# Attention over short sequences: working 32 heads at a time instead of 16, with 8 KB runs for Q, K and the output

## The chip, the cores and the metric

The kernel runs on one core of a Trainium2 chip. The metric is the device time of one execution in microseconds, given as the median of several executions.

## The reference

There are 32 x 12 = 384 independent heads. Each has Q, K and V of 128 rows by 64 columns in f32. For each head the output is softmax(Q K^T / 8) V, with the softmax taken along the rows:

```python
scale = 1.0 / np.sqrt(q.shape[-1])
scores = scale * np.matmul(q, k.transpose(0, 1, 3, 2))
scores_max = np.max(scores, axis=-1, keepdims=True)
attn = np.exp(scores - scores_max)
attn = attn / (np.sum(attn, axis=-1, keepdims=True) + 1e-8)
return np.matmul(attn, v).astype(np.float32)
```

Q, K and V are 12.6 MB each and the output is 12.6 MB, all of it moved once. The kernels here leave the maximum out (the scores are small) and divide by the sum at the end.

## The kernel before

A **chunk** is 16 heads; there are 24 chunks. A chunk of Q is loaded as 128 partitions of `TQ` = 16 rows each, so each partition reads one contiguous run of 16 x 64 f32 = 4 KB. These loads come from GpSimd's queue (line 58 for Q and K), which turns f32 into bf16 on the way, so that 2 KB is written for each run of 4 KB. V is loaded by line 65, in runs of 2 KB, 32 heads for each DMA. Only the first chunk's Q and K come as f32 over the SP and ACT queues (line 81) and are cast by VectorE and ScalarE (line 83).

The steps for chunk c are these:

- `turn` (lines 107 and 109, VectorE): 32x32 block transposes put the head dimension of Q and K on the partitions. A pair of bf16 values is moved as one f32, so one chunk is 512 columns for each of Q and K.
- `scores` (line 120, TensorE, 32 matmuls) into `s_ps`, which is one slot of four PSUM banks, and the exponential of all 2048 columns (line 124, ScalarE) into `attn`.
- `values` (line 139, TensorE, then a copy by ScalarE, line 143): V's rows are brought into the order that the turned keys have, by matmuls with a permutation matrix `perm`.
- `denominators` (line 149) and `divide` (lines 171 and 173): sums over the keys by a matmul with ones, turned back by a VectorE transpose, and the reciprocal.
- `outputs` (line 159, twice per chunk, 16 matmuls each) and `finish` (line 178, VectorE): the transposed output in PSUM is turned back into `o_sb`.
- `scale_rows` (line 183, GpSimd): `o_sb` times the reciprocal. For the last chunk VectorE takes half (line 186).
- `store` (line 191): `o_sb` to HBM in runs of 4 KB, issued by ScalarE's queue, and by SP's for the last three chunks.

`d_ps`, `o_ps` and `v_ps` share `w_ps`: four slots of one PSUM bank.

The order of the instructions on each engine is written out by hand (`tc.manual_schedule()`); each engine works through its own list in order, and waits on semaphores for the others. The GpSimd queue uses eight semaphores in turn for its loads, so a load waits until the one eight before it has landed. Loads run `AHEAD` = 7 chunks ahead, and stores are held back by `LAG` = 9 chunks (the list `held`), so that the loads come first and the stores follow when the loads thin out. The main loop:

```python
for c in range(NCH):
    todo = shuffles.get(c, [])
    if c < e:
        turn(c + 1, 0)
        turn(c + 1, 1)
    d_ps = denominators(c)
    if c < e:
        scores(c + 1)
    divide(c, d_ps)
    finish(c, 0, outputs(c, 0))
    ...
```

The functions that the change touches:

Of the kernel before, what the change touches and what calls it, by code (L numbers as in the profile page):

```python
# [10 lines left out]
def kernel(  # L11
# [10 lines left out]

    nc = tc.nc
    f32 = mybir.dt.float32
# [5 lines left out]
    TQ = 16  # L30
    GQ = S // TQ
# [3 lines left out]
    NCH = B * H // 16  # L35
    AHEAD = 7
    LAG = 9
# [8 lines left out]
    pin = ctx.enter_context(tc.tile_pool(name="pin", bufs=AHEAD + 3))  # L46
    pt = ctx.enter_context(tc.tile_pool(name="pt", bufs=3))
    pa = ctx.enter_context(tc.tile_pool(name="pa", bufs=3))
    pf = ctx.enter_context(tc.tile_pool(name="pf", bufs=8))
# [5 lines left out]
    def load_qk(c):  # L55
        for src, which in ((qr, 0), (kr, 1)):
            x = pin.tile([128, TQ, D], bf16, tag="qk"[which] + "_bf", name="qk"[which] + "_bf")
            nc.gpsimd.dma_start(out=x, in_=src[:, c, :].rearrange("p (t d) -> p t d", t=TQ))  # L58
            chunks[c, which] = x
# [9 lines left out]
    with tc.manual_schedule():  # L69
        early = {0: 0, 1: 1, 2: 2, 3: 3, 4: 4, 5: 5}  # L70
        early.update({4 * m - 5 + i: 2 * m + i for m in range(3, NCH // 4) for i in range(2)})

        def load(c):
            load_qk(c)
            if c in early:
                load_v(early[c])

        for src, which, eng, cast in ((qr, 0, nc.sync, nc.vector.tensor_copy),
                                      (kr, 1, nc.scalar, nc.scalar.copy)):
            raw = po.tile([128, TQ, D], f32, tag="o_sb", name="raw")  # L80
            eng.dma_start(out=raw, in_=src[:, 0, :].rearrange("p (t d) -> p t d", t=TQ))
            x = pin.tile([128, TQ, D], bf16, tag="qk"[which] + "_bf", name="qk"[which] + "_bf")
            cast(x, raw)  # L83
            chunks[0, which] = x
        load_qk(1)
        load_v(early[0])
        ident = singles.tile([128, 128], bf16)
        make_identity(nc, ident)
        load_v(early[1])
        perm = singles.tile([128, A, 2, 32], bf16)  # L90
        nc.vector.memset(perm, 0.0)
        for tl in range(2):
            nc.vector.tensor_copy(
                perm[:, :, tl, tl * 16:(tl + 1) * 16].rearrange("p a (x g) -> p a x g", x=2),
                ident.rearrange("p (a g x) -> p a x g", a=A, x=2))
        ones = singles.tile([128, 32], bf16)
        nc.vector.memset(ones, 1.0)
        for c in range(2, AHEAD):
            load(c)

        def turn(c, which):


            x = chunks.pop((c, which)).bitcast(f32)
            xt = pt.tile([128, 4, S], f32, tag="qk"[which] + "t", name="qk"[which] + "t")
            if which == 0:
                nc.vector.transpose(xt.rearrange("p h (x g) -> p x h g", g=GQ), x)  # L107
            else:
                nc.vector.transpose(xt.rearrange("p h (x g) -> p x h g", g=GQ),  # L109
                                    x.rearrange("p (y t) e -> p t y e", y=2))  # L110
            qts[c, which] = xt.bitcast(bf16).rearrange("p h (s j) -> p h s j", j=2)

        def scores(c):
            qt, kt = qts.pop((c, 0)), qts.pop((c, 1))
            s_ps = ps.tile([128, 4, 4, S], f32, tag="s_ps", name="s_ps")
            for h in range(4):
                for j in range(2):
                    for b in range(4):
                        pr = slice(b * 32, (b + 1) * 32)
                        nc.tensor.matmul(  # L120
                            s_ps[:, b, h, :], lhsT=kt[pr, h, :, j], rhs=qt[pr, h, :, j],
                            start=(j == 0), stop=(j == 1), tile_position=(b * 32, 0))
            attn = pa.tile([128, 4, 4, S], bf16, tag="attn", name="attn")
            nc.scalar.activation(out=attn, in_=s_ps, func=mybir.ActivationFunctionType.Exp,  # L124
                                 bias=0.0, scale=scale)
            attns[c] = attn

        def values(m, a, heads, half):


            v_bf = chunks[m, 2]
            ns = slice(0, 2 * CB) if half is None else slice(half * CB, (half + 1) * CB)
            if m not in v2s:
                v2s[m] = pa.tile([128, A, 2 * CB, D], bf16, tag="v2", bufs=2, name="v2")
            v_ps = ps.tile([128, heads, 2 * CB // heads, D], f32, tag="w_ps", bufs=4, name="v_ps")
            for i in range(heads):
                for tl in range(2):
                    for u in range(4):
                        nc.tensor.matmul(  # L139
                            v_ps[u * 32:(u + 1) * 32, i], lhsT=perm[:, a + i, tl, :],  # L140
                            rhs=v_bf[:, ns, 2 * u + tl, :], start=(tl == 0), stop=(tl == 1),
                            tile_position=(0, u * 32))
            nc.scalar.copy(v2s[m][:, a:a + heads, ns], v_ps)  # L143

        def denominators(c):

            d_ps = ps.tile([128, 4, S], f32, tag="w_ps", bufs=4, name="d_ps")
            for b in range(4):
                nc.tensor.matmul(  # L149
                    d_ps[b * 32:(b + 1) * 32], lhsT=ones, rhs=attns[c][:, b],  # L150
                    start=True, stop=True, tile_position=(0, b * 32))
            return d_ps

        def outputs(c, j):

            o_ps = ps.tile([128, 4, S], f32, tag="w_ps", bufs=4, name="o_ps")
            for h in range(4):
                for b in range(4):
                    nc.tensor.matmul(  # L159
                        o_ps[b * 32:(b + 1) * 32, h],  # L160
                        lhsT=v2s[c // 4][:, 4 * (b % 2) + h, 2 * (c % 4) + b // 2,
                                         j * 32:(j + 1) * 32],
                        rhs=attns[c][:, b, h], start=True, stop=True, tile_position=(0, b * 32))
            return o_ps

        def turned(src):
            return src.rearrange("p h (x g) -> p x h g", g=GQ)

        def divide(c, d_ps):
            dt = pf.tile([128, TQ, 32], f32, tag="dt", name="dt")  # L170
            nc.vector.transpose(dt, turned(d_ps))  # L171
            recip = pf.tile([128, TQ], f32, tag="recip", name="recip")
            nc.vector.reciprocal(recip, dt[:, :, 0])  # L173
            osbs[c] = (po.tile([128, TQ, D], f32, tag="o_sb", name="o_sb"), recip)

        def finish(c, j, o_ps):
            o_sb, _ = osbs[c]
            nc.vector.transpose(o_sb[:, :, j * 32:(j + 1) * 32], turned(o_ps))  # L178

        def scale_rows(c):  # L180
            o_sb, recip = osbs[c]
            if c < NCH - 1:
                nc.gpsimd.tensor_mul(o_sb, o_sb, recip.to_broadcast([128, TQ, D]))  # L183
            else:
                for eng, sl in ((nc.gpsimd, slice(0, 32)), (nc.vector, slice(32, 64))):
                    eng.tensor_mul(o_sb[:, :, sl], o_sb[:, :, sl],  # L186
                                   recip.to_broadcast([128, TQ, 32]))

        def store(c, eng):
            o_sb, _ = osbs.pop(c)  # L190
            eng.dma_start(out=orr[:, c, :], in_=o_sb.rearrange("p t d -> p (t d)"))

        e = NCH - 1
        held = {c: [c - LAG] if c >= LAG else [] for c in range(e - 4)}
        held[e - 4] = [e - 13, e - 12]
        held[e - 3] = [e - 11, e - 10, e - 9]
        held[e - 2] = [e - 8, e - 7, e - 6]
        held[e - 1] = [e - 5, e - 4, e - 3]
        held[e] = [e - 2, e - 1, e]
        shuffles = {c: [(c // 4 + 1, 2 * (c % 4) + i, 1, None) for i in range(2)]  # L200
                    for c in range(4, NCH - 4)}
        for c in range(2):
            shuffles[c] = [(0, 4 * c + 2 * i, 2, 1) for i in range(2)]
            shuffles[c + 2] = [(1, 4 * c + i, 1, None) for i in range(4)]
        turn(0, 0)
        turn(0, 1)
        scores(0)
        for a in range(0, A, 2):
            values(0, a, 2, 0)
        for c in range(NCH):  # L210
            todo = shuffles.get(c, [])
            if c < e:
                turn(c + 1, 0)
                turn(c + 1, 1)
            d_ps = denominators(c)
            if c < e:
                scores(c + 1)
            divide(c, d_ps)
            finish(c, 0, outputs(c, 0))
            for x in todo[:len(todo) // 2]:  # L220
                values(*x)
            finish(c, 1, outputs(c, 1))
            for x in todo[len(todo) // 2:]:
                values(*x)
            if c + AHEAD < NCH:
                load(c + AHEAD)
            scale_rows(c)
            for s in held[c]:
                store(s, nc.scalar if s < e - 2 else nc.sync)
# [30 lines left out]
```

The softmax here doesn't subtract the row's maximum and nothing guards it: scores larger than these inputs give would overflow.

## Time and profile before

| | |
|---|---|
| median of 5 runs | 130.53 us (130.51 to 130.86) |
| the profiled execution's own time | 130.51 us |
| span in the profile, first to last instruction | 128.7 us |
| mean granted TensorE clock | 0.849 |
| busy: TensorE, VectorE, ScalarE, GpSimd | 55%, 67%, 56%, 62% |
| loads on the GpSimd queue | 58 DMAs (23 Q, 23 K, 12 V) |
| stores | 24 DMAs of 0.52 MB |
| HBM read and written | 37.75 MB and 12.58 MB |

The profiled execution has 1.8 us outside the span. In the page, the row "DMA" in the 40 slices is the mean busy share of the 16 DMA engines, in tenths, and "GB/s" is what they wrote. A load that casts f32 to bf16 reads two bytes for each byte it writes, so 208 GB/s of such loads are 416 GB/s read. In the groups of instructions, "idle before" is the time that the engine stood still just before them, with what ended most of it.

### The profile page before, as it was taken

The page shows a single profiled execution, that of the slowest core. Times are in us where ns is not written, and L with a number is a line of the kernel's source. Part 1 is how long each engine was busy: PE and PEld are TensorE (multiplying, and loading weights), DVE is VectorE, ACT ScalarE, POOL GpSimd, SP SyncE. Part 2 cuts the span into 40 slices and gives each one's busy share as a digit, 9 for nine tenths or more (in the row PEclk, how much of TensorE's full clock was granted, in tenths as well). Part 3 has the DMA queues.
Part 4 walks back from the last instruction along what each step waited for, and adds up shares of the span by engine and source line. Part 5 has one row for each costly group of instructions (what it writes and reads, how often), then busy time and mean ns, then how long its engine had stood idle before and what let it go on. Part 6 is the DMA issues. An engine that isn't in the chain of part 4 may idle for free.

```text
span 128.7 us, 4637 instructions
## 1 busy us (share of the span) xinstructions
PE 70.9 (55%) x2080; PEld 43.6 (34%) x2080; DVE 85.8 (67%) x150; ACT 71.9 (56%) x74; POOL 79.7 (62%) x88
## 2 busy tenths in 40 slices
PE   0034965597646754665676486193956665666000
PEld 0024744344323432344244244060633333544000
DVE  0290297648879698957899559355599997786700
ACT  3116778557948745873777295353547885324000
POOL 6961314335699986998756577818999743454400
PEclk9999999859999999996799769855599999655555
DMA  3999999999999999999999999999999999999982
GB/s 110 308 177 202 208 210 205 210 214 201 214 205 210 205 214 207 207 210 210 283 246 280 253 286 218 275 286 211 272 224 287 276 269 335 397 419 413 420 367 89
DMA packets 16723, 32.27 MB, mean 251 GB/s; under 512 B 1344, under 2 KB 7488, under 8 KB 16704
## 3 DMA queue, kind: packets, MB, share of 16 engines
q0 software_dynamic: 12960, 18.35, 80.0%
q10 hardware_dynamic: 3168, 11.54, 23.0%
q1 hardware_dynamic: 576, 2.10, 4.3%
q8 instruction: 16, 0.26, 0.7%
q14 instruction: 3, 0.02, 0.0%
HBM read 37.75 MB, written 12.58 MB: 391 GB/s over the span
## 4 chain that ended last, share of the span: by engine, by line
DMA 58%; DVE 12%; POOL 11%; PE 7%; issue 4%; ACT 1%; POOLq 0%; DVEq 0%; ACTq 0%
DMA k_bf<-in_k_dram 22%; DMA q_bf<-in_q_dram 22%; DMA v_bf<-in_v_dram 11%; DVE o_sb L178 6%; POOL o_sb L183 4%; PE s_ps L120 4%; DMA out_dram<-o_sb 3%; POOL v_bf L65 3%; DVE kt L109 3%; DVE qt L107 2%; POOL q_bf L58 2%; PE o_ps L159 2%; ACT attn L124 1%; POOL k_bf L58 1%; DVE o_sb L186 1%
## 5 line engine op out<-in xcount | busy, mean ns | idle before, releaser
L124 ACT ACTIVATE attn<-s_ps 128x2048 bf16<-128x2048 f32 x24 | 45.0, 1877 | 37.2 <-PE s_ps L120 34.9
L183 POOL TENSOR_TENSOR o_sb<-o_sb,recip 128x1024 f32<-128x1024 f32 x23 | 44.0, 1913 | 9.5 <-DVE o_sb L178 9.3
L178 DVE STREAM_TRANSPOSE o_sb<-o_ps 128x512 f32<-128x512 f32 x48 | 33.1, 711 | 15.5 <-PE o_ps L159 14.6
L139 PE MATMUL v_ps<-v_bf,perm 128*32 128x512 bf16 (+1 forms) x448 | 34.5, 411 | 4.8 <-DMA v_bf<-in_v_dram 3.6
L120 PE MATMUL s_ps<-qt,kt 32*128 32x128 bf16 x768 | 18.2, 240 | 32.1 <-DVE kt L109 32.0
L143 ACT CAST v<-v_ps 128x512 bf16<-128x512 f32 x48 | 26.5, 589 | 3.7 <-PE v_ps L139 3.7
L120 PEld LDWEIGHTS <-kt 32*128 32x128 bf16 x768 | 13.4, 104 | 41.0 <-DVE kt L109 40.6
L159 PE MATMUL o_ps<-attn,v 128*32 128x128 bf16 x768 | 22.7, 249 | 2.0 <-issue 2.0
L58 POOL DMA_DIRECT2D k_bf<-in_k_dram x23 | 12.3, 533 | 15.0 <-DMA v_bf<-in_v_dram 10.2
L171 DVE STREAM_TRANSPOSE dt<-d_ps 128x512 f32<-128x512 f32 x24 | 16.3, 679 | 6.5 <-PE d_ps L149 6.4
L159 PEld LDWEIGHTS <-v 128*32 128x32 bf16 x768 | 15.9, 110 | 11.2 <-issue 6.6
L109 DVE STREAM_TRANSPOSE kt<-k_bf 128x512 f32<-128x512 f32 x24 | 16.3, 680 | 5.0 <-DMA k_bf<-in_k_dram 5.0
L58 POOL DMA_DIRECT2D q_bf<-in_q_dram x23 | 13.4, 584 | 7.5 <-DMA v_bf<-in_v_dram 3.9
L107 DVE STREAM_TRANSPOSE qt<-q_bf 128x512 f32<-128x512 f32 x24 | 16.3, 678 | 1.0 <-DMA q_bf<-in_q_dram 1.0
L149 PE MATMUL d_ps<-attn,ones 128*32 128x512 bf16 x96 | 10.5, 412 | 9.1 <-ACT attn L124 9.1
L139 PEld LDWEIGHTS <-perm 128*32 128x32 bf16 x448 | 12.4, 114 | 7.7 <-issue 5.7
L65 POOL DMA_DIRECT2D v_bf<-in_v_dram x12 | 9.3, 777 | 8.3 <-PE o_ps L159 2.4
L149 PEld LDWEIGHTS <-ones 128*32 128x32 bf16 x96 | 4.4, 100 | 15.2 <-issue 12.7
L173 DVE RECIPROCAL recip<-dt 128x16 f32<-128x16 f32 x24 | 6.1, 254 | 1.9
L83 DVE CAST q_bf<-raw 128x1024 bf16<-128x1024 f32 x1 | 0.7, 695 | 5.7 <-DMA raw<-in_q_dram 5.7
L83 ACT CAST k_bf<-raw 128x1024 bf16<-128x1024 f32 x1 | 1.0, 1045 | 3.4 <-DMA raw<-in_k_dram 3.4
L83 ACT ACT_TABLE_LOAD x1 | 1.3, 1283 | 1.2 <-PEq L244 1.2
(11 smaller groups left out, 3.8 us busy)
## 6 DMA issues: line engine op xcount, KB each, us to landing
out_dram<-o_sb ACTq DMA_DIRECT2D x21, 512.0 KB, 7.2
v_bf<-in_v_dram POOLq DMA_DIRECT2D x12, 512.0 KB, 13.7
q_bf<-in_q_dram POOLq DMA_DIRECT2D x23, 256.0 KB, 12.9
k_bf<-in_k_dram POOLq DMA_DIRECT2D x23, 256.0 KB, 12.9
out_dram<-o_sb SPq DMA_DIRECT2D x3, 512.0 KB, 6.5
raw<-in_k_dram ACTq DMA_DIRECT2D x1, 512.0 KB, 5.1
raw<-in_q_dram SPq DMA_DIRECT2D x1, 512.0 KB, 4.9
```

Of the source, the lines that this page charges most:

```text
L58: nc.gpsimd.dma_start(out=x, in_=src[:, c, :].rearrange("p (t d) -> p t d", t=TQ))
L107: nc.vector.transpose(xt.rearrange("p h (x g) -> p x h g", g=GQ), x)
L109: nc.vector.transpose(xt.rearrange("p h (x g) -> p x h g", g=GQ), x.rearrange("p (y t) e -> p t y e", y=2))
L120: nc.tensor.matmul(s_ps[:, b, h, :], lhsT=kt[pr, h, :, j], rhs=qt[pr, h, :, j], start=(j == 0), stop=(j == 1), tile_position=(b * 32, 0))
L124: nc.scalar.activation(out=attn, in_=s_ps, func=mybir.ActivationFunctionType.Exp, bias=0.0, scale=scale)
L139: nc.tensor.matmul(v_ps[u * 32:(u + 1) * 32, i], lhsT=perm[:, a + i, tl, :], rhs=v_bf[:, ns, 2 * u + tl, :], start=(tl == 0), stop=(tl == ...
L143: nc.scalar.copy(v2s[m][:, a:a + heads, ns], v_ps)
L149: nc.tensor.matmul(d_ps[b * 32:(b + 1) * 32], lhsT=ones, rhs=attns[c][:, b], start=True, stop=True, tile_position=(0, b * 32))
L159: nc.tensor.matmul(o_ps[b * 32:(b + 1) * 32, h], lhsT=v2s[c // 4][:, 4 * (b % 2) + h, 2 * (c % 4) + b // 2, j * 32:(j + 1) * 32], rhs=attn ...
L171: nc.vector.transpose(dt, turned(d_ps))
L178: nc.vector.transpose(o_sb[:, :, j * 32:(j + 1) * 32], turned(o_ps))
L183: nc.gpsimd.tensor_mul(o_sb, o_sb, recip.to_broadcast([128, TQ, D]))
```

## The change

A unit of work is now a **duo** of 32 heads; there are 12 of them. Only `scores` and the exponential still work on 16 heads at a time, so they are called twice per duo, as `scores(m, 0)` and `scores(m, 1)`. What differs:

- Q, K and output run 8 KB per partition (`TQ` = 32). Each of these DMAs moves 1.05 MB on the f32 side instead of 0.52 MB. V's loads are as they were.
- `turn`, `divide` and `finish` are transposes of 1024 columns; `values` copies 1024 columns at a time; `scale_rows` multiplies 2048 columns.
- `w_ps` is two slots of two PSUM banks instead of four slots of one.
- The first duo's casts are split between VectorE and ScalarE.
- Loads are named in an explicit order (`load("v0 q1")`, `later`), 5 duos of Q and K have buffers, and stores wait 5 duos (`LAG` = 5).
- `turn(m + 2)` stands at the end of stage m; before, `turn(c + 1)` stood at the beginning of stage c.
- Stores of duos 0 to 7 stand in ScalarE's list, at the end of a stage; duos 8, 9 and 10 are stored by SP, which has nothing else to do, and the last duo in two halves by ScalarE and SP.

The number of matmuls does not change. The diff, cut to its core:

```diff
-    TQ = 16
-    GQ = S // TQ
+    TQ = 32
...
-    NCH = B * H // 16
-    AHEAD = 7
-    LAG = 9
+    NDUO = B * H // 32
+    AHEAD = 5
+    LAG = 5
...
-    pin = ctx.enter_context(tc.tile_pool(name="pin", bufs=AHEAD + 3))
-    pt = ctx.enter_context(tc.tile_pool(name="pt", bufs=3))
-    pa = ctx.enter_context(tc.tile_pool(name="pa", bufs=3))
-    pf = ctx.enter_context(tc.tile_pool(name="pf", bufs=8))
+    pin = ctx.enter_context(tc.tile_pool(name="pin", bufs=AHEAD))
+    pt = ctx.enter_context(tc.tile_pool(name="pt", bufs=2))
+    pa = ctx.enter_context(tc.tile_pool(name="pa", bufs=4))
+    pf = ctx.enter_context(tc.tile_pool(name="pf", bufs=2))
     po = ctx.enter_context(tc.tile_pool(name="po", bufs=LAG + 3))
...
+        load("v0 q1")
         ident = singles.tile([128, 128], bf16)
         make_identity(nc, ident)
-        load_v(early[1])
+        load("k1 v1")
...
+        for which in range(2):
+            raw = chunks[0, which]
+            x = pin.tile([128, TQ, D], bf16, tag="qk"[which] + "_bf", name="qk"[which] + "_bf")
+            nc.vector.tensor_copy(x[:, :TQ // 2], raw[:, :TQ // 2])
+            nc.scalar.copy(x[:, TQ // 2:], raw[:, TQ // 2:])
+            chunks[0, which] = x
+        load("q2 k2 v2 v3 q3 k3 v4 v5 q4 k4")
+        later = ["q5 k5", "v6 v7 q6 k6", "q7 k7", "v8 v9 q8 k8", "q9 k9", "v10 v11 q10 k10",
+                 "q11 k11"]
...
-            v_ps = ps.tile([128, heads, 2 * CB // heads, D], f32, tag="w_ps", bufs=4, name="v_ps")
+            v_ps = ps.tile([128, heads, 4 * CB // heads, D], f32, tag="w_ps", bufs=2, name="v_ps")
...
-            d_ps = ps.tile([128, 4, S], f32, tag="w_ps", bufs=4, name="d_ps")
+            d_ps = ps.tile([128, 8, S], f32, tag="w_ps", bufs=2, name="d_ps")
...
-            o_ps = ps.tile([128, 4, S], f32, tag="w_ps", bufs=4, name="o_ps")
+            o_ps = ps.tile([128, 8, S], f32, tag="w_ps", bufs=2, name="o_ps")
...
+        e = NDUO - 1
+        held = {m: [m - LAG] for m in range(LAG, e - 2)}
+        held[e - 2], held[e - 1] = [e - 7, e - 6], [e - 5, e - 4]
+        shuffles = {0: [(0, 0, 4, 1), (0, 4, 4, 1)],
+                    1: [(1, a, 2, None) for a in range(0, A, 2)]}
+        for m in range(2, NDUO // 2):
+            shuffles[2 * m - 2] = [(m, 0, 2, None)]
+            shuffles[2 * m - 1] = [(m, a, 2, None) for a in range(2, A, 2)]
         turn(0, 0)
         turn(0, 1)
-        scores(0)
+        scores(0, 0)
+        values(0, 0, 4, 0)
+        scores(0, 1)
+        values(0, 4, 4, 0)
+        turn(1, 0)
+        turn(1, 1)
+        for m in range(NDUO):
+            todo = shuffles.get(m, [])
+            if m < e:
+                scores(m + 1, 0)
+            divide(m, denominators(m))
+            if len(todo) > 3:
+                values(*todo.pop(0))
+            finish(m, 0, outputs(m, 0))
+            if len(todo) > 1:
+                values(*todo.pop(0))
+            if m < e:
+                scores(m + 1, 1)
+            finish(m, 1, outputs(m, 1))
+            for x in todo:
+                values(*x)
+            if m + 2 <= e:
+                turn(m + 2, 0)
+                turn(m + 2, 1)
+            if m < len(later):
+                load(later[m])
+            if m < e:
+                scale_rows(m, nc.gpsimd, 0, TQ)
+                for s in held.get(m, []):
+                    store(s, nc.scalar)
+            else:
+                scale_rows(m, nc.vector, 0, TQ // 2)
+                scale_rows(m, nc.gpsimd, TQ // 2, TQ)
+                for s in range(e - 3, e):
+                    store(s, nc.sync)
+                store(m, nc.scalar, 0, TQ // 2)
+                store(m, nc.sync, TQ // 2, TQ)
```

## The prediction

> **What bounds the kernel now.** I read the 40 slices first, then the queues, the chain, and the groups.
>
> ```profile
> span 128.7 us, 4637 instructions
> DMA  3999999999999999999999999999999999999982
> GB/s 110 308 177 202 208 210 205 210 214 201 214 205 210 205 214 207 207 210 210 283 246 280 253 286 218 275 286 211 272 224 287 276 269 335 397 419 413 420 367 89
> DMA 58%; DVE 12%; POOL 11%; PE 7%; issue 4%; ACT 1%; POOLq 0%; DVEq 0%; ACTq 0%
> ```
>
> The DMA row is at 9 from the second slice to the 38th. The casting loads write 205 to 214 GB/s, so read about 418; the stores alone reach 410 to 420. So the 16 DMA engines are full from about 2 us until 3 us before the end, and no compute engine is busy over 67% of the span. All traffic is 50.3 MB (37.75 read, 12.58 written); at 418 GB/s that is 120.4 us, and 2.2 us of start, 1.4 us after the last byte, instruction fetches and small losses make 128.7. **So the time is the DMA's work plus whatever time the DMA stands idle.** Compute matters only where it lets the DMA run dry. The change is to be judged by two questions: does it make the DMA's work shorter, and does the DMA still always have something to move?
>
> **The DMA's work.** Q, K and output packets grow from 4 KB to 8 KB on the f32 side. What does a packet cost beside its bytes? A stretch with only V (2 KB read per packet) and one with only Q and K (4 KB):
>
> ```profile
> DMA packets 801, 0.80 MB, mean 201 GB/s; under 512 B 16, under 2 KB 801, under 8 KB 801
> ...
> DMA packets 340, 0.63 MB, mean 210 GB/s; under 512 B 33, under 2 KB 33, under 8 KB 340
> ```
>
> V: 1024 B written at 201/16 GB/s is 81.5 ns a packet; Q and K: 2048 B at 210/16 is 156 ns. Twice the first less the second leaves 7 ns for a packet as such. Packets of 4 KB: 46 x 128 of Q and K, 256 raw, 24 x 128 stores, 9216 in all or 576 per engine; half of them go, 288 x 7 ns = 2.0 us. The Trainium skill (DMA: Bandwidth & Descriptors, section "Why small descriptors are slow") gives about 3 cycles of fixed overhead per packet, at 850 MHz 3.5 ns: an estimate of 1.0 us. No row shows 8 KB, and if such runs were cut to 4 KB the gain is 0. I take 1.4 us, between the two, and keep 0 to 2.0 (a loss I exclude: going from 2 to 4 KB helped). Bytes are the same. Without idle time the span is 128.7 - 1.4 = **127.3**.
>
> **Does the DMA run dry at the start or in the middle?** The first Q and K are 1.05 MB each, so the first scores start near 12 us instead of 8.4; costs nothing, because eight loads of 1.05 MB (20 us of DMA) can be in flight on GpSimd's queue. Its later loads stand ahead of `scale_rows(m)`, each waits for the one eight before it, and so about six are always in flight. Nothing of GpSimd's list makes the DMA wait. If that cover were gone, each load would cost up to its 2.5 us.
>
> The compute rows, doubled in width:
>
> ```profile
> L124 ACT ACTIVATE attn<-s_ps 128x2048 bf16<-128x2048 f32 x24 | 45.0, 1877 | 37.2 <-PE s_ps L120 34.9
> L183 POOL TENSOR_TENSOR o_sb<-o_sb,recip 128x1024 f32<-128x1024 f32 x23 | 44.0, 1913 | 9.5 <-DVE o_sb L178 9.3
> L143 ACT CAST v<-v_ps 128x512 bf16<-128x512 f32 x48 | 26.5, 589 | 3.7 <-PE v_ps L139 3.7
> 99.89 1.37 DVE o_sb L178 x2
> 101.26 0.59 DVE qt L107
> 90.34 1.04 PE L120 MATMUL s_ps<-qt,kt 32*128 32x128 bf16 x32 [2.26 <-DVE kt L109]
> 95.22 0.64 PE L120 MATMUL s_ps<-qt,kt 32*128 32x128 bf16 x32 [1.32 <-DVE kt L109]
> ```
>
> ScalarE: 512 columns 0.59 us, 2048 1.88, so 1024 by a straight line 1.02. VectorE: a turn of 512 takes 0.59 of the chain, a finish 0.68; for 1024 I take 1.15 and 1.25 (bounds: the columns alone 1.07, twice the old 1.37). GpSimd: 512 columns took 1.04 (line 186), 1024 1.91, so 2048 3.65. Matmul counts stay: scores 0.64 us, `outputs` of 32 0.80, `denominators` 0.80, `values` of 16 1.2, at the full clock. With these a stage's VectorE list (two turns, dt, reciprocal 0.35, two finishes) is 6.5 us, and with the waits on the two PSUM slots and on the single `s_ps` slot a stage lasts 7.8 us with one `values` and 8.9 with three, 8.3 on average (before, 3.65 per chunk, 7.3 per duo: two slots are slower than four). The loads of a duo take 3 x 2.5 = 7.5 us, with a store 10. So once stores run, compute waits for loads: slack, and no cost.
>
> **Where it does run dry: stage 9.** Stores 4 and 5 stand in ScalarE's list at the end of stage 9, behind the exponential of `scores(10, 1)` and three `values` copies. VectorE's list puts `turn(10)` ahead of all of stage 9, so stage 9 cannot start before k10 has landed. After k10 the queue holds only q11 and k11. Stores 0 to 3 came at the ends of stages 5 to 8; SP's store 8 needs only `scale_rows(8)`.
>
> Count from the start of stage 8. k9 landed some 2.6 us before. v10, v11, q10, k10 are 10.2 us of DMA. Store 2 is issued at about 0; a store beside loads first moves 3.9 us after its issue (first store issued at 57.90; from there to 61.7 its queue shows 17 packets):
>
> ```profile
> q10 hardware_dynamic: 17, 0.07, 4.8%
> raw<-in_q_dram SPq DMA_DIRECT2D x1, 512.0 KB, 4.9
> ```
>
> So loads run alone to 3.9 (6.5 done), share with store 2 until 8.9 (2.5), and k10 lands at 10.2. Store 3 (issued 6.5) moves from 10.4, store 8 (finishes end at 5.5, GpSimd 3.65, issued 9.2) from 13.1. **From k10's landing the DMA thus has q11, k11 and stores 3 and 8: 10.1 us of work.**
>
> Stage 9 from k10's landing: turn of K with its wait 1.25; then scores(10, 0) 1.04, denominators 1.3 (to 2.3), dt 1.2 (3.5, frees a slot), `values` 1.4 (4.9), scores(10, 1) 0.65, its exponential behind the first copy, 5.95 to 7.85, two copies to 9.95: 11.2 us. Then store 4 is issued. A transfer that meets empty engines needs 2.35 us to its first byte (raw Q: 4.9 us for landing, of which 1.05 MB of raw Q and K move in 2.55). Store 4's first byte is at 13.55; **the DMA is idle for 13.55 - 10.1 = 3.5 us.**
>
> Here TensorE's clock speaks against the change. The row at 90.34 has scores at 1.04 us after 2.26 us idle, against 0.64 at 95.22. The Trainium skill (TensorE: Matmul & The Clock Gate, Part 1) says that an idle window of about 3.4 us halves the clock; the trace halved it after a shorter gap. TensorE stands about 6 us before stage 9, so both give the slow clock. With the full clock the chain would be 1.05 us shorter and the idle time 2.4 us.
>
> How sure is 3.5? If k9 lands just before stage 8, k10 lands at 12.6, store 3 has moved 1.1 us of its work before, and idle is 4.6. If loads are 2.5 us further ahead, VectorE sets stage 9's start instead and store 2's rest is still to move: 1.3 at the least. So 1.3 to 4.6.
>
> **Afterwards**, stores 4, 5, 6, 7, 9, 10, 11 remain, 7.3 MB, 17.7 us. Is DMA or compute last? From k10 turned (T0): stage 9's finishes end at 7.6, turn(11) 9.9, exp(11, 0) 12.6, exp(11, 1) 15.2, denominators and dt 17.2, reciprocal and two finishes 20.1, half the multiplication on VectorE 2.1 (512 columns took 1.10): issue at 22.2, landing at T0 + 27.2. DMA: T0 + 12.3 + 17.7 = 30.0. DMA is last, by 2.8 us (about 1.5 if the slow clock holds). Stores 6, 7 (15.2), 9 (11.3), 10 (19.0) are in time to keep it full.
>
> Sum: 127.3 + 3.5 = 130.8 span. The profiled execution was 130.51 with a span of 128.7, so 1.8 outside (and 0.02 below the median of 130.53): **132.6 us**.
>
> **The rivals.**
> *A, faster: the DMA never runs dry.* If store 4's first byte comes within 10.1 us of k10's landing, only the packets count: 127.3 + 1.8 = 129.1 (128.5 to 130). For it: the present stores are spread so that the slices never dip. Against: stage 9's chain alone is 11.2. It would need 3.5 us less, of ScalarE's copies and slot waits.
> *B, VectorE becomes the bound.* Compute's slack is small: at 8.3 a stage, stage 9 could start at 17.8 (end of the first duo's exponentials) + 9 x 8.3 = 92.5, against about 99 by the loads (37 of the 48 transfers of 1.05 MB are through by then); 0.7 us more per stage and compute leads. Writing in pieces of 4 columns instead of 8 could do that; against it, Q's and K's turns cost the same (678 and 680 ns) though their reads differ. At 9.8 a stage: stage 9 at 106, plus 31.4 is 137.4, or 139 us.
> *C, the change does not do what it says:* 8 KB runs move as 4 KB ones. Then 132.6 + 1.4 = 134.0.
>
> **How the numbers follow.** Forecast 0.58, A 0.18, B 0.12, C 0.12. Forecast's own range: gain 0 to 2.0 and idle 1.3 to 4.6 give 129.8 to 135.1. Low end 129.3 leaves out half of A; high end 136 takes in C with the longest idle and leaves out most of B: about 2 in 10 outside. A change under 0.2% (0.26 us) can't be told from none here. Slower: the forecast but for its low corner, B, C, 0.76; same 0.05 (idle near 1.4); faster 0.19.
>
> **What would show it.** Right: GB/s shows a dip of 3 to 4 us near 106 to 112 us, just ahead of store 4; TensorE idle about 6 us on `kt` before stage 9; seven stores (17.7 us at 410 to 420) after the dip; Q and K stretches at 212 to 214 GB/s. The idle step is wrong if the DMA row stays at 9 to the end; the packet step if Q and K stretches stay at 210; the compute step if `finish` of 1024 columns is over 1.4 us or stages last over 9.

## The result and the profile after

The changed kernel takes 131.61 us (median of 20 executions, 130.36 to 132.81), the kernel before 130.64 (39 executions, 130.32 to 130.94). The ratio is 1.0059, with a 95% interval of 1.0042 to 1.0076: slower by some 0.8 us by the ratio, 1.0 by the medians. Ratios leave out executions that lie more than 1.5% above the fastest of their kernel (2 of 20 here, 4 of 10 for the third trace of the changed kernel below, 1 of 14 for the short burst), and as a kernel whose executions spread loses its longest ones by that, the medians stand where the two differ. The forecast was 132.6: the right direction and inside the range, but with 2.1 us of loss, twice what was measured or more.

The traced execution was the longest of the 20, 132.81 us, with a span of 131.0. The page's slices (busy tenths of the 16 DMA engines, and GB/s written):

```profile
span 131.0 us, 4462 instructions
DMA  4999999999999999999999999999999953999990
GB/s 98 403 256 207 199 214 215 204 213 213 200 214 217 215 202 209 217 215 208 206 210 218 211 304 271 366 211 217 265 315 280 379 188 160 425 403 415 410 405 35
```

Between the first slice and the last, the DMA row leaves 9 in one place, the 33rd and 34th slices (5 and 3; 105 to 111 us). After it five slices of stores alone at 403 to 425. The same place closer, 103 to 112 us in 40 bins of 0.225 us:

```profile
DMA  9998998997548534434310000000000969967995
GB/s 437 400 382 346 382 455 364 401 419 328 164 164 291 182 146 182 164 146 182 146 73 36 36 0 0 0 0 0 0 0 0 510 255 400 583 255 328 583 473 218
```

The rate falls to half at 105.3 us, to nothing at 108.2, and the next store's first bytes come at 110.0. What is late there is on the chain that ended last (start, length, what; the lines up to the dots) and in ScalarE's list (the lines behind them):

```profile
70.22 28.49 DMA k_bf<-in_k_dram
98.73 1.25 DVE kt L107
99.98 0.05 issue
100.03 1.04 PE s_ps L119 x28
101.07 1.00 PE d_ps L150 x8
102.10 1.26 DVE dt L172
103.36 0.04 issue
103.40 1.90 PE v_ps L139 x16
...
106.35 1.88 ACT L124 ACTIVATE attn<-s_ps 128x2048 bf16<-128x2048 f32 x1
108.12 2.13 ACT L143 CAST v<-v_ps 128x1024 bf16<-128x1024 f32 x2
109.25 0.82 ACTq L188 DMA_DIRECT2D out_dram<-o_sb  x2
```

K of duo 10 lands at 98.7 and is turned by 99.98; scores, denominators, dt, `values`, the second exponential and the copies follow one another, and stores 4 and 5 go out at 109.25. The groups of the changed kernel show that the wider instructions cost what was assumed (idle before them at the right):

```profile
L183 POOL TENSOR_TENSOR o_sb<-o_sb,recip 128x2048 f32<-128x2048 f32 x11 | 39.9, 3623 | 26.6 <-DVE o_sb L179 22.7 <-issue 3.9
L179 DVE STREAM_TRANSPOSE o_sb<-o_ps 128x1024 f32<-128x1024 f32 x24 | 28.9, 1215 | 12.5 <-PE o_ps L160 12.5
L143 ACT CAST v<-v_ps 128x1024 bf16<-128x1024 f32 x24 | 24.1, 1015 | 13.7 <-PE v_ps L139 13.6
L107 DVE STREAM_TRANSPOSE kt<-k_bf 128x1024 f32<-128x1024 f32 x12 | 14.5, 1209 | 2.1 <-DMA k_bf<-in_k_dram 2.1
```

VectorE, ScalarE and GpSimd are all less busy than before (78, 71 and 64 us against 86, 72 and 80), and the kernel is slower. None of them was the bound.

### The profile page after: what moved, and what is told of

The parts are those of the page before. It is cut to its first block, busy times and chain, and to the rows that moved or that the text cites. A ratio compares the mean times of both kernels' runs of the same rounds, so it can differ in the third digit from the quotient of the medians.

```text
span 131.0 us, 4462 instructions
## 1 busy us (share of the span) xinstructions
PE 70.7 (54%) x2080; PEld 42.3 (32%) x2080; DVE 77.8 (59%) x79; ACT 70.7 (54%) x51; POOL 64.4 (49%) x52
## 3 DMA queue, kind: packets, MB, share of 16 engines
q0 software_dynamic: 9504, 17.83, 73.1%
## 4 chain that ended last, share of the span: by engine, by line
DMA 64%; POOL 7%; DVE 7%; PE 6%; issue 5%; ACT 3%; POOLq 2%; ACTq 0%; DVEq 0%
DMA v_bf<-in_v_dram 43%; DMA k_bf<-in_k_dram 22%; POOL o_sb L183 4%; ACT attn L124 3%; DVE o_sb L179 3%; PE s_ps L119 3%; POOLq L263 2%; DVE dt L172 2%; DVE kt L107 2%; PE v_ps L139 1%; PE d_ps L150 1%; POOL k_bf L57 1%; POOL v_bf L65 1%; DVE qt L107 1%; POOL q_bf L57 1%
## 5 line engine op out<-in xcount | busy, mean ns | idle before, releaser
L124 ACT ACTIVATE attn<-s_ps 128x2048 bf16<-128x2048 f32 x24 | 45.1, 1879 | 23.6 <-PE s_ps L119 23.6
L183 POOL TENSOR_TENSOR o_sb<-o_sb,recip 128x2048 f32<-128x2048 f32 (+1 forms) x12 | 42.7, 3562 | 29.5 <-DVE o_sb L179 25.6
L179 DVE STREAM_TRANSPOSE o_sb<-o_ps 128x1024 f32<-128x1024 f32 x24 | 28.9, 1215 | 12.5 <-PE o_ps L160 12.5
L143 ACT CAST v<-v_ps 128x1024 bf16<-128x1024 f32 x24 | 24.1, 1015 | 13.7 <-PE v_ps L139 13.6
L172 DVE STREAM_TRANSPOSE dt<-d_ps 128x1024 f32<-128x1024 f32 x12 | 15.0, 1249 | 20.1 <-PE d_ps L150 20.1
L160 PE MATMUL o_ps<-attn,v 128*32 128x128 bf16 x768 | 18.2, 241 | 1.8 <-issue 0.9
L107 DVE STREAM_TRANSPOSE kt<-k_bf 128x1024 f32<-128x1024 f32 x12 | 14.5, 1209 | 2.1 <-DMA k_bf<-in_k_dram 2.1
L107 DVE STREAM_TRANSPOSE qt<-q_bf 128x1024 f32<-128x1024 f32 x12 | 14.5, 1208 | 1.7 <-DMA q_bf<-in_q_dram 1.7
L57 POOL DMA_DIRECT2D q_bf<-in_q_dram x11 | 6.1, 554 | 14.0 <-DMA v_bf<-in_v_dram 11.5
L57 POOL DMA_DIRECT2D k_bf<-in_k_dram x11 | 5.9, 541 | 12.4 <-DMA v_bf<-in_v_dram 7.5
L174 DVE RECIPROCAL recip<-dt 128x32 f32<-128x32 f32 x12 | 4.2, 353 | 0.8
```

Source lines behind the costliest of these rows:

```text
L57: nc.gpsimd.dma_start(out=x, in_=(qr, kr)[which][:, m, :].rearrange("p (t d) -> p t d", d=D))
L107: nc.vector.transpose(xt.rearrange("p h (x g) -> p x h g", g=4), x if which == 0 else x.rearrange("p (y t) e -> p t y e", t=T))
L160: nc.tensor.matmul(o_ps[b * 32:(b + 1) * 32, h], lhsT=v2s[m // 2][:, h, 4 * (m % 2) + b, j * 32:(j + 1) * 32], rhs=attns[m, h // 4][:, b, ...
L183: eng.tensor_mul(o_sb[:, lo:hi], o_sb[:, lo:hi], recip[:, lo:hi].to_broadcast([128, hi - lo, D]))
```

## The experiments

One theory and three rivals stood at the start. **Theory 1:** the DMA runs dry in stage 9, from the end of the loads to store 4, and this dry time is all of the loss. **Rivals:** VectorE's longer stages set the end; or the tail does; or 8 KB runs bring nothing.

### Stores 4 and 5 earlier

```diff
             if m < e:
                 scores(m + 1, 0)
+            if m == e - 2:
+                for s in held.pop(m):
+                    store(s, nc.scalar)
             divide(m, denominators(m))
```

> Stores 4 and 5 move on ScalarE's list from the end of stage 9 to just behind the exponential of scores(10, 0). Theory 1: the dry stretch is gone, the median falls by its whole length until the tail of the computation ends it: 129.2 to 130.4 us, faster than before's 130.6, and the executions lie closer together. Rival 1 (VectorE's longer stages are the bound): within 0.3 us of 131.6. Rival 2 (q11 and k11 are now late and stage 10 waits for them): 131 to 132.

Measured: 128.98 us (128.56 to 130.33), ratio to the kernel before 0.9879 (0.9842 to 0.9917). Its stores go out at 100.67, and from 103 to 110 us the bins of its trace are full; from 110.4 to 111.5 they fall to about half:

```profile
100.67 0.90 ACTq L188 DMA_DIRECT2D out_dram<-o_sb  x2
...
DMA  8998799989898998999898989998999986654986
GB/s 328 382 528 346 273 455 401 455 328 437 328 473 328 437 437 364 437 473 437 364 473 364 510 364 437 437 473 364 473 401 401 401 328 291 255 218 182 583 364 291
```

Nothing was taken away and nothing shortened; two DMA issues moved some 8 us up one engine's list, and 3.1 us went (132.11, below, for the unchanged kernel on the same chip). The place of these two stores caused the loss. VectorE's work is the same, so rival 1 falls. VectorE turned k11 without a wait, so rival 2 falls too. The median is below the range that was expected by 0.2 us. The executions did not lie closer together, as was expected: 1.8 us apart over six, against 0.5 over five of the unchanged kernel beside it. It is the quickest of the complete kernels here, and quicker than the kernel before: with the dry stretch gone, the rest of the change pays.

### The changed kernel again

> The changed kernel once more, for a second trace. Theory 1 (the DMA runs dry in stage 9, for as long as the chain from k10's landing to store 4 lasts, and that chain is 1 us longer when TensorE runs at half clock): the median stays near 131.6 us, single executions between 130.4 and 132.8, and if this trace's execution is near 131 us its dry stretch is about 1.5 to 2.4 us instead of 3.4. Rival (the executions differ for a reason elsewhere, in the tail): the dry stretch has the same 3.4 us whatever the time.

Measured beside it, without an edit: 132.11 us (131.78 to 132.28), ratio 1.0102 (1.0085 to 1.0119). Its traced execution took 132.28; store 4 went out at 108.80. It lies too close to the first trace to tell the theory from its rival.

### The transfers alone, in 8 KB and in 4 KB runs

Both kernels leave out all computation; the output is a constant. Their core, with `TQ` 32 or 16:

```diff
+        o_sb = po.tile([128, TQ, D], f32, tag="o_sb", name="o_sb")
+        nc.vector.memset(o_sb, 1.0)
...
+        for m in range(12):
+            for i in range(R):
+                if R * m + i:
+                    load_qk(R * m + i)
+            load_v(m)
+        for n in range(N):
+            (nc.scalar, nc.sync)[n % 2].dma_start(
+                out=orr[:, n, :], in_=o_sb.rearrange("p t d -> p (t d)"))
```

> All of the transfers of the changed kernel and none of its computation: Q, K and output in runs of 8 KB, V in runs of 2 KB, the same casts, with the stores (of a constant) issued from the start on ScalarE's and SP's queues. Theory 1 (without a dry stretch the changed kernel's time is the transfers' own, 129.1 us): 127.5 to 129.5 us. Rival (8 KB runs are no quicker than 4 KB ones): the same as the next kernel within 0.3 us.

> The same transfers without computation in runs of 4 KB, as in the kernel before. Theory 1 (7 ns of each packet are its own, halved with the bigger runs): 1 to 2 us above the kernel with 8 KB runs, the forecast's 1.4. Rival: within 0.3 us of it.

Measured: 128.32 us (128.19 to 128.37) and 131.61 us (131.31 to 131.93). The difference of 3.3 us is more than the theory or the rival said, but not all of it is bytes. From 120 to 130 us in bins of 0.25 us, first 8 KB, then 4 KB:

```profile
GB/s 213 197 246 180 201 135 205 205 209 217 205 209 201 197 135 107 4 0 0 0 0 0 0 0 0 0 0 0 0 0 0 0 0 0 0 0 0 0 0 0
...
GB/s 229 180 213 213 213 213 197 213 213 205 205 188 197 205 205 221 209 205 209 193 152 98 25 0 0 0 0 0 0 0 0 0 0 0 0 0 0 0 33 0
```

The loads' last bytes come in the 17th bin (124.3) and in the 23rd (125.8): 1.5 us, against the forecast's 1.4. The rival that 8 KB runs bring nothing falls. The 4 KB kernel then has nearly four more microseconds to the end of its span of 129.6, the 8 KB one 2.3 to 126.6; what the rest of that is was not tried. So a whole time of these two kernels is no floor: with 4 KB runs the transfers alone (131.61) took longer than the kernel before with all its computation (130.67 on this chip). That the kernel with early stores (128.98) lies within 0.7 us of the transfers alone in 8 KB runs does not show how much is left to win.

### One microsecond more in front of store 4

```diff
             nc.scalar.copy(v2s[m][:, a:a + heads, ns], v_ps)
+            if (m, a) == (5, 6):
+                nc.scalar.copy(v2s[m][:, a:a + heads, ns], v_ps)
```

> The changed kernel with the last copy of stage 9 on ScalarE done twice, so that stores 4 and 5 are issued 1.0 us later and nothing else is: a measure of what a microsecond of that wait costs. Theory 1: the dry stretch and the time grow by 0.9 to 1.1 us over the changed kernel on the same chip. Rival (the end is set by VectorE's and ScalarE's tail, stores 4 and 5 have room): 0 to 0.3 us.

> The changed kernel once more, as the measure for the kernel with the longer stage and for a further trace. Theory 1: if its traced execution is near 131 us, the dry stretch is shorter by what the time is shorter, and stage 9's first matmuls run at the full clock; if it is near 132.2, as in the traces so far, they run at half.

Measured: 132.27 us (131.04 to 132.63), ratio 1.0108 (1.0078 to 1.0139), against 131.74 (130.17 to 132.64), ratio 1.0033 (1.0005 to 1.0060), for the unchanged kernel beside it. By the ratios that is 0.75%, 1.0 us; by the medians it is 0.5 us, between the theory's 0.9 to 1.1 and the rival's 0 to 0.3. The executions spread over 1.6 and 2.5 us, so the medians decide nothing. In the two traces the issue of store 4 is 109.30 against 108.21 and the time 132.63 against 131.72: 1.1 us later, 0.9 us longer.

This trace also settles the rival of the tail. GpSimd's last multiplication, which the last store waits for, stands in the changed kernel's first trace and in this one as

```profile
122.25 2.89 POOL L183 TENSOR_TENSOR o_sb<-o_sb,recip 128x1024 f32<-128x1024 f32 x1 [2.91 <-DVE o_sb L179]
...
119.48 2.89 POOL L185 TENSOR_TENSOR o_sb<-o_sb,recip 128x1024 f32<-128x1024 f32 x1 [1.09 <-DVE o_sb L181]
```

The computation ends 2.8 us earlier here, and the execution takes the same time (132.63 against 132.81), with store 4 issued at 109.30 against 109.25. The end follows store 4 and not the computation.

The expectation for the unchanged kernel's trace was half wrong: at 131.72 its first scores still ran at the slow clock (1.04 us), and the clock came up within the stage (granted 0.53 in the first 5 us after k10 was turned, 1.00 in the next 4).

### TensorE kept busy in front of stage 9

The first try repeats half of `scores(9)` five times:

```diff
             for x in todo:
                 values(*x)
+            if m == e - 3:
+                warm(m + 1, 5)
```

> At the end of stage 8 TensorE repeats a half of scores(9) five times, 160 extra matmuls into the free s_ps slot that nobody reads; they fill some 3.5 us in which it otherwise stands. Theory 1: stage 9 starts at the full clock, its chain is 1 us shorter, the dry stretch is about 2.4 us at most: median 130.5 to 131.0 us and few executions over 131.5. Rival (the clock has no part in it): 131.4 to 131.8 with the same spread.

Measured: 137.17 us (136.35 to 137.97), ratio 1.0489. The theory and the rival both missed; the trace says why:

```profile
96.61 1.19 PE L135 MATMUL warm_ps<-qt,kt 32*128 32x128 bf16 x69 [0.53 <-ACT attn L124]
99.84 2.64 PE L135 MATMUL warm_ps<-qt,kt 32*128 32x128 bf16 x91 [2.05 <-issue]
102.55 1.04 PE L119 MATMUL s_ps<-qt,kt 32*128 32x128 bf16 x32
```

After 69 of the 160 extra matmuls TensorE stood for 2.05 us with nothing to wait for that the trace shows, came back at half clock (granted 1.00 in the first part of the burst, 0.50 in the second), and began stage 9 at 102.55 instead of 100.03. Store 4 went out at 113.10. As a test of the clock it failed; as a second dose of lateness it is useful below.

> Both edits together: stores 4 and 5 early in stage 9, and the 160 extra matmuls at the end of stage 8. Theory 1: once the stores are early the clock in stage 9 no longer sets any dry stretch, only the tail of the computation: within 0.5 us of the kernel with early stores alone, 129 to 130.2 us. Rival (the clock of stages 10 and 11 is what spreads the times): 1 us less than with early stores alone.

Measured: 135.11 us (134.46 to 135.49), ratio 1.0327. The burst again stood 2.60 us and stage 9 began at 103.58, so stores 6 and 7 came late instead (118.72 against 112.61 with early stores alone: 6.1 us, as much as the medians are apart). The expectation, within 0.5 us of early stores alone, was missed; the run says nothing on the clock.

The second try is 24 matmuls of 512 columns, 48 instructions instead of 320:

```diff
+            if m == e - 3:
+                warm(m, 24)
...
+                nc.tensor.matmul(
+                    s_ps[b * 32:(b + 1) * 32, b], lhsT=ones, rhs=attns[m, 1][:, b],
+                    start=True, stop=True, tile_position=(0, b * 32))
```

> A second try at keeping TensorE's clock up in front of stage 9: 24 extra matmuls of 512 columns at the end of stage 8 (some 2.4 us at the full clock, 48 instructions instead of 320), into the free s_ps slot, read by nobody. Theory 1: stage 9's first scores take 0.64 us instead of 1.04, store 4 is issued about 8 us after k10 is turned instead of 8.6 to 9.25, and the time is 0.6 to 1.2 us less than the changed kernel's beside it. Rival (the clock has no part): the same within 0.3 us. If the extra matmuls end after k10 is turned, the time is longer by what they are late.

> The changed kernel once more, as the measure for the kernel with the short burst. Theory 1 also says that an execution's time is the issue of store 4 plus a constant: in the traces so far, 109.25, 108.80 and 108.21 us went with 132.81, 132.28 and 131.72 us, so the constant is 23.5 us; here it should be 23.3 to 23.7 again. Rival (the spread comes from the tail): the constant varies with the time.

Measured: 130.78 us (130.22 to 132.19), ratio 1.0015 (0.9998 to 1.0033), against 131.14 (130.66 to 132.41), ratio 1.0051 (1.0029 to 1.0073), unchanged beside it. By the ratios that is 0.36% less, 0.5 us, and the two intervals overlap; by the medians it is 0.4 us. That is less than the 0.6 to 1.2 expected, and hardly more than the rival's 0.3. The stage, first with the burst and then without, in TensorE's and ScalarE's lists:

```profile
99.08 0.64 PE L119 MATMUL s_ps<-qt,kt 32*128 32x128 bf16 x32 [0.91 <-DVE kt L107]
101.61 1.05 PE L147 MATMUL v_ps<-v_bf,perm 128*32 128x512 bf16 x16 [0.80 <-DVE dt L180]
107.05 2.46 ACTq L196 DMA_DIRECT2D out_dram<-o_sb  x2
...
99.93 0.64 PE L119 MATMUL s_ps<-qt,kt 32*128 32x128 bf16 x32 [4.10 <-DVE kt L107]
102.47 1.90 PE L139 MATMUL v_ps<-v_bf,perm 128*32 128x512 bf16 x16 [0.59 <-DVE dt L172]
108.02 0.82 ACTq L188 DMA_DIRECT2D out_dram<-o_sb  x2
```

With the burst the clock stays up through the stage (granted 1.00, `values` 1.05 us). Without it this execution happened to start at the full clock too, and dropped behind the first scores (granted 0.66 in the first 5 us, `values` 1.90). But the stage gained little by it: of the 0.97 us between the two issues of store 4, 0.85 are there because k10 was turned earlier (99.03 against 99.88), and only 0.12 lie in the chain behind. So this pair of traces does not show that the burst's gain comes from the clock.

### All traces together

| traced execution | time, us | k10 turned | granted clock, next 5 us | store 4 issued | stage 9's chain | time less issue |
|---|---|---|---|---|---|---|
| changed kernel, first | 132.81 | 99.98 | 0.50 | 109.25 | 9.27 | 23.56 |
| changed kernel, second | 132.28 | 99.87 | 0.50 | 108.80 | 8.93 | 23.48 |
| changed kernel, third | 131.72 | 99.57 | 0.53 | 108.21 | 8.64 | 23.51 |
| changed kernel, fourth | 131.54 | 99.88 | 0.66 | 108.02 | 8.14 | 23.52 |
| one copy more | 132.63 | 99.45 | 0.52 | 109.30 | 9.85 | 23.33 |
| long burst | 136.54 | 99.57 | 0.50 | 113.10 | 13.53 | 23.44 |
| short burst | 130.51 | 99.03 | 1.00 | 107.05 | 8.02 | 23.46 |
| stores early | 129.05 | 99.84 | 0.66 | 100.67 | | 28.38 |

"Stage 9's chain" is the time from k10 turned to the issue of store 4. Over 6 us of lateness an execution's time is that issue plus 23.3 to 23.6 us, as was expected before the fourth trace. Only the kernel with early stores falls out, as it must: there the DMA does not stop at this place. The kernel with both edits is left out, as its store 4 is early and its stores 6 and 7 are late. In the four traces of the changed kernel the chain is the shorter, the higher the clock (the first two differ in the 4 us after these five, 0.86 and 0.96); four traces and one short burst are too few to say how much of it the clock makes.

## Why the prediction was right or wrong

**The bound: right.** The time is the DMA's work plus its idle time. All compute engines got less busy and the kernel slower.

**The packets: right.** 1.4 us was forecast, between the 2.0 from the trace's 7 ns a packet and the 1.0 worked out from the 3 cycles of the Trainium skill (DMA: Bandwidth & Descriptors, "Why small descriptors are slow"). The transfers alone gave 1.5 us by their last bytes, some 5 ns for each of the 288 packets that an engine was spared, so between the two figures. The kernel with early stores came to 128.98 where rival A's sum had 129.1. A stretch of Q and K alone, 70.5 to 76 us, wrote 218 GB/s with a few stores' packets among them; before it was 210. Without the stores' packets and their time I estimate 213, inside the forecast's 212 to 214.

**The place: right, the wait for k10 too long.** The DMA ran dry in stage 9, between the loads' end and store 4, and moving only those two stores took the loss away: they stand at the end of ScalarE's list. That k10 holds up VectorE's list is the smaller part of the reason:

```profile
98.73 1.25 DVE L107 STREAM_TRANSPOSE kt<-k_bf 128x1024 f32<-128x1024 f32 x1 [0.96 <-DMA k_bf<-in_k_dram]
100.03 1.04 PE L119 MATMUL s_ps<-qt,kt 32*128 32x128 bf16 x32 [3.75 <-DVE kt L107]
```

In the first trace k10 landed 7.6 us after stage 8 began (its scores start at 91.13), not 10.2. VectorE waited 0.93 to 1.63 us for it in the four traces, and hardly at all with the early stores or the short burst. TensorE stood 3.73 to 4.41 us before stage 9, not 6. So the slow clock was less sure than the prediction took it to be: three of the four executions began the stage at it, and one, after 4.10 us, at the full clock. The row at 90.34 of the kernel before, which the prediction took for a clock halved by a gap of 2.26 us, was misread: the clock had been granted at 0.50 since 84 us, ahead of that gap. Its scores at 73.10 do show it after 1.92 us: granted 1.00 until 72.5, 0.50 from 73.1.

**The idle time, the term that was mis-sized.** The forecast had 3.5 us. The kernel with early stores against the changed one gives 131.61 - 128.98 = 2.6 us at the medians, and 3.1 on one chip. The step that failed is stage 9's chain: "its exponential behind the first copy, 5.95 to 7.85, two copies to 9.95 ... Then store 4 is issued". From k10 turned to the issue the traces have 9.27, 8.93, 8.64 and 8.14, not 9.95, for two reasons. The first is clear from each trace: the issue does not wait for the copies to end. Store 4's 109.25 lies inside the 2.13 us of the last two copies, as the last one starts, 1.0 us ahead of its end; in the other three traces it is 1.0 to 1.1 us. The second is argued from the table: the chain is longest where the granted clock is lowest, and it was not at half for the same time in each execution.

With the constant of 23.5 us, the median of 131.61 is store 4 at 108.1. The idle time of such an execution can be estimated from the first trace, with k10 landing at 98.7, 0.75 us from issue to first bytes and 7.6 us of work (both below): 9.4 + 0.75 - 7.6 = 2.6 us, as the early stores show it. The forecast had 11.2 + 2.35 - 10.1. All three terms were too long: the first by 1.8 us, and the other two work against each other and leave 0.9.

The forecast's own figure for the full clock, 2.4 us of idle time, gives 131.5, next to the median. That is luck: in all four traces the clock was low for a part of the stage, and it is the early issue that alone makes the chain 1.0 us shorter.

**Errors that cancelled.** In the first trace the whole sum comes out (span 130.8 forecast, 131.0 measured), but not for its own reasons. "The DMA thus has q11, k11 and stores 3 and 8: 10.1 us of work" was too much. From k10's landing to the first bytes of store 4, 98.7 to 110.3 us, the queues moved:

```profile
q10 hardware_dynamic: 161, 1.18, 24.7%
q0 software_dynamic: 156, 0.54, 23.1%
q1 hardware_dynamic: 144, 1.05, 21.8%
```

That is 1.08 MB read by loads (0.54 written), 1.05 of store 8, and some 1.05 of store 3 (1.18 less the first of store 4): 3.2 MB, 7.6 us at 418 GB/s. So q11 and k11 were half done when k10 was seen to land. Why that is so, and why the rate stands at half for 3 us before it stops, is open: engines that finish apart would fit both, but no view here shows single engines. On the other side, "2.35 us to its first byte" was too long: issue 109.25, first bytes 110.0, 0.75 us. Idle in that trace is 110.0 - 98.7 - 7.6 = 3.7 us, with a chain of 9.27 us where 9.95 was forecast.

**The rivals.** A is what the kernel becomes once two stores are moved. B fell: finishes took 1.215 us, turns 1.21, where 1.25 and 1.15 were taken, so pieces of 4 columns do not make them long, and VectorE's work did not set the time once the stores were early. C fell with the transfers alone.

## What to carry to other kernels

When DMA is the bound, a store's place in the list of the engine that issues it is part of the bandwidth: count what the queues still hold when the last load lands, and let the next store be issued before that runs out, not at the end of a stage that waits for the load. Coarser stages can make this worse, since a whole stage of work then stands between a landing and the next issue. And when you add up such a chain, end it where the trace shows the issue: here it went out as the copy ahead of it in the list started, 1.0 us before that copy ended.

## What was not expected of the hardware

TensorE stands for 1 to 2.6 us in full traffic with nothing to wait for that the trace shows: 2.05 us in the long burst, 2.60 with both edits, and in the changed kernel's tail (115.76 and then 117.74, the same group of eight denominators):

```profile
115.76 0.38 PE L150 MATMUL d_ps<-attn,ones 128*32 128x512 bf16 x1 [0.86 <-ACT attn L124]
...
117.74 0.40 PE L150 MATMUL d_ps<-attn,ones 128*32 128x512 bf16 x3 [1.60 <-issue]
```

The stop in the tail is in all four traces of the changed kernel (1.60, 1.32, 1.06 and 0.98 us) and in none with early stores, one copy more or a burst. It did not set the time: the execution with one copy more had no such stop and was as long as the first.

In the first trace and in the long burst's, the "instruction" queue has one packet of 0.02 MB near the stop: between 115.4 and 115.5 us in the changed kernel, between 97.5 and 98 us in the long burst. That would fit a fetch of the next instructions that stands in line behind data, but it was seen together, not tested. If so, matmuls added to fill a gap have a price that the gap does not show.

The other surprise is the spread. Executions of the changed kernel lie over 2.4 us, those of the kernel before over 0.6. In the four traces the time goes with the issue of store 4, so the dry stretch passes on whatever varies ahead of it, the clock among it. It is not all of the spread: six executions of the kernel with early stores still lie over 1.8 us, one of them alone at 130.33 and the rest from 128.56 to 129.33. Why is open.
